# Pairing the spilled U-block outputs of a PEER feed-forward: one tile, one DRAM place and one transfer for two blocks

## The chip, the cores and the metric

The kernel runs on 1 core of one Trainium2 chip. The metric is the device time of one execution in microseconds (us). The kernel before the change was timed three times; the profile is one further execution, taken by the hardware profiler. TensorE does the matrix products (PE in the profile, its weight loads PEld), VectorE and ScalarE (DVE, ACT) the element-wise work, GpSimd (POOL) issues the gathers and SyncE (SP) issues most transfers. SP executes nothing but its issues, strictly in the order of the program: an issue that waits holds all that stand behind it.

## The reference

The reference is one layer of an encoder on 512 tokens of width 1024: two kinds of attention, a projection, a layer norm, and then a PEER feed-forward, a sigmoid gate and a last layer norm. The change touches the PEER part alone:

```python
q = (xb @ w_q).reshape(PEER_CHUNK, PEER_HEADS, PEER_KEY_DIM)
s1 = jnp.einsum('thd,kd->thk', q[..., :half], sub_keys[0])
s2 = jnp.einsum('thd,kd->thk', q[..., half:], sub_keys[1])
v1, i1 = lax.top_k(s1, PEER_TOPK)
v2, i2 = lax.top_k(s2, PEER_TOPK)
...
idx = (e1 * PEER_N_KEYS + e2).reshape(PEER_CHUNK, PEER_HEADS * PEER_TOPK)
g = jax.nn.softmax(cv.astype(jnp.float32), axis=-1).reshape(PEER_CHUNK, -1).astype(xb.dtype)
u = u_table[idx]
hpre = jnp.einsum('td,ted->te', xb, u)
act = g * jax.nn.gelu(hpre, approximate=False)
return jnp.einsum('te,ted->td', act, v_table[idx])
```

Each token picks 128 of 16384 experts (8 heads, 16 each). Expert e has a row of `u_table` and a row of `v_table`, each of 1024 numbers. The result of a token is the sum, over its picks, of the pick's weight g times gelu(token . u row) times the v row.

## The kernel before, in words

**Dense and gathered tokens.** For the first 128 tokens the picked rows are gathered, one row for each token and pick (lines 1351 and 1366), and VectorE does the products (lines 1357 and 1368). For the other 384 tokens (`N_D`) the kernel multiplies with all experts: it scatters the weights g into a dense table (128 blocks of 128 experts, `g_dram`, line 1024), and multiplies that table, times the gelu of the U products, with all of V. Of those 384, the U products of 128 (`N_S`) are gathered earlier as well (`own_rows`), so that the U blocks are made for 256 tokens (`N_U`).

**The lead stage** (415 to 900 us of the profile). For U blocks 0 to 99 (`LEAD`) `lead_block` multiplies one block of U rows with the 256 tokens (line 1150), beside the routing and the building of the dense table; `leave_u` takes the gelu on ScalarE (line 1132) into a tile of 128 experts x 256 tokens, 128 KB. Blocks 0 to 87 (`SPILL`) are then stored in DRAM by ScalarE's own queue (line 1134, `ge_dram`). Blocks 88 to 95 (`KEPT`) stay in tiles of another pool, and blocks 96 to 99 stay in tiles named `ge`. In this stage the order of the work is written out by hand on all engines: a planner (`run_pe`) interleaves matrix products with VectorE's steps by their costs.

**The output stage** (900 to 1518 us). The main loop takes the 128 blocks in the order 88 to 127, then 0 to 87; n is the place in that order. In this loop VectorE's and SP's orders are those of the program; ScalarE's and TensorE's are set by the scheduler that builds the kernel. For place n:

- SP issues, in this order, quarters of the next group's dense table (`load_g`, line 1321; 384 KB each, four for 8 blocks, from place 40 on at n % 8 = 6, 6, 7 and 7), V's block n (`load_v`, line 1336; 512 KB), and the gelu tile `GE_AHEAD` = 3 places on (line 1427; 128 KB; from place 37 to place 124).
- VectorE multiplies the table's block with the gelu tile (line 1432); ScalarE and VectorE split V's block and the product into two parts of fewer bits (lines 99 and 100: `v_hi`, `v_lo` or `whi`, `wlo`, and `a_hi`, `a_lo`).
- TensorE adds 18 products of 128x128 with 128x512 into six accumulators (line 1383).
- At places 8 to 35, `expert_in` makes U block n + 92 (100 to 127), whose gelu tile (line 805) is used four places later.
- VectorE and GpSimd do some of the gathered tokens' rows.

**Buffers.** The name `ge` has `GES` = 9 tiles of 128 x 256 numbers, used in turn by the lead stage, by `expert_in` and by the loads of line 1427. V's blocks have three tiles of `v_raw` and, at odd places from 37 to 123, three of `raw`, so that from place 37 on a load of V waits for the split six places before. The halves `v_hi`, `v_lo`, `a_hi`, `a_lo` have two tiles each.

Of the kernel before, what the change touches and what calls it, by code (L numbers as in the profile page):

```python
# [9 lines left out]
F32 = mybir.dt.float32  # L10
# [4 lines left out]
AF = mybir.ActivationFunctionType  # L15
# [17 lines left out]
N_U = N_D - N_S  # L33
# [3 lines left out]
SPILL = 88  # L37
# [19 lines left out]
NA_FROM = (0, 64, 192, 256)  # L57
GATS = 8
NO_GATHER = 1
GE_AHEAD = 3  # L60
GES = 9
RAWS = 4
LOW = -3.0e38
FEED_NA = 3.1
# [8 lines left out]
def tile_encoder_layer(ctx: ExitStack, tc: tile.TileContext, A: dict, out: bass.AP):  # L73
    nc = tc.nc
# [6 lines left out]
    dram = ctx.enter_context(tc.tile_pool(name="dram", bufs=1, space=bass.MemoryType.DRAM))  # L81
# [14 lines left out]
    def split(hi, lo, src, scale=None):  # L96

        if scale is None:
            nc.scalar.copy(hi, src)  # L99
            nc.vector.tensor_tensor(lo, src, r32(hi), op=OP.subtract)  # L100
        else:
            nc.scalar.mul(hi, src, scale)
            nc.vector.scalar_tensor_tensor(lo, src, scale, r32(hi), op0=OP.mult, op1=OP.subtract)

    def stream(src, shape, scale=None):
        raw = wst.tile([128] + shape, F32, name="raw", bufs=3)
        nc.sync.dma_start(raw, src)
        hi = wst.tile([128] + shape, F32R, name="whi")
        lo = wst.tile([128] + shape, F32R, name="wlo")
        split(hi, lo, raw, scale)  # L110
        return hi, lo

    def mm3(ps, a, b, start, stop):
        nc.tensor.matmul(ps, a[0], b[0], start=start, stop=False)  # L114
        nc.tensor.matmul(ps, a[0], b[1], start=False, stop=False)  # L115
        nc.tensor.matmul(ps, a[1], b[0], start=False, stop=stop)  # L116
# [55 lines left out]
    def ps_tile(name, bufs=2):  # L172
        return ps6.tile([128, 512], F32, name=name, bufs=bufs)
# [102 lines left out]
    with tc.tile_pool(name="ln0", bufs=1, reuse_waits="tile") as ln0, \  # L276
# [16 lines left out]
        for kk in range(4):  # L293
            raw = wst.tile([128, 2, 512], F32, name="raw", bufs=3) if kk < 3 else ln0.tile([128, 2, 512], F32,
                                                                                         name="vraw3")
# [465 lines left out]
    for c in range(4):  # L761
        cs = slice(c * 128, (c + 1) * 128)
        ps = ps_tile("pj")
# [8 lines left out]
    for c in range(4):  # L772
        cs = slice(c * 128, (c + 1) * 128)
        ps = ps_tile("mm")
# [10 lines left out]
    NTG = N_D // GT  # L785
    ts = slice(T - N_U, T)
    u_rows, v_rows = A["u_rows"], A["v_rows"]
    ge_dram = dram.tile([SPILL, 128, N_U], F32, name="ge_dram")
    g_dram = dram.tile([NTG, 128, 128 * GT], F32, name="g_dram")

    pB = ctx.enter_context(tc.tile_pool(name="pB", bufs=1, reuse_waits="tile"))
# [3 lines left out]
    hdot = pB.tile([128, NGC, 128], F32, name="hdot")  # L795
    ge_t = {}

    def expert_in(i):

        ps = psH.tile([128, 512], F32, name="hp")  # L800
        u = stream(A["uT"][i], [8, 128])
        for k in range(8):
            mm3(ps[:, :N_U], (u[0][:, k], u[1][:, k]), (hTh[:, k, ts], hTl[:, k, ts]), k == 0, k == 7)
        ge = pB.tile([128, N_U], F32, name="ge", bufs=GES)
        nc.scalar.activation(ge, ps[:, :N_U], AF.Gelu)
        if i < SPILL:
            nc.sync.dma_start(ge_dram[i], ge)
        else:
            ge_t[i] = ge


    pX = ctx.enter_context(tc.tile_pool(name="pX", bufs=1, reuse_waits="tile"))
# [52 lines left out]
    for g in range(16):  # L865
# [5 lines left out]
        ps = ps_tile("mm", 4)  # L871
# [251 lines left out]
    def leave_u(i, ps):  # L1123
        k = i - SPILL
        if 0 <= k < KEPT:
            if k % 2 == 0:
                name = ("g_raw", "g_raw", "g_hi", "g_lo")[k // 2]
                kept.append(pK.tile([128, 2, N_U], F32, name=name, bufs=2 if k < 4 else 1))
            ge = kept[k // 2][:, k % 2]
        else:  # L1130
            ge = pB.tile([128, N_U], F32, name="ge", bufs=GES)
        nc.scalar.activation(ge, ps[:, :N_U], AF.Gelu)  # L1132
        if i < SPILL:
            nc.scalar.dma_start(ge_dram[i], ge)
        else:
            ge_t[i] = ge

# [71 lines left out]
    def gate_and_leads():  # L1209
# [37 lines left out]
        if last:  # L1247
            leave_u(*last.pop())
# [60 lines left out]
    order = list(range(SPILL, 128)) + list(range(SPILL))  # L1309
    pV = ctx.enter_context(tc.tile_pool(name="pV", bufs=1, side="right", reuse_waits="tile"))  # L1310

    def load_g(n, q, t):

        i = order[n]
        if q == 0:
            if n // GB % 2 == 0:
                t = pX.tile([128, NTG, GB, GT], F32, name="gt1")
            else:
                t = pV.tile([128, NTG, GB, GT], F32, name="gt0")
        g = slice(q * NTG // 4, (q + 1) * NTG // 4)  # L1320
        nc.sync.dma_start(t[:, g].rearrange("p g i t -> p g (i t)"),
                          g_dram[g, :, i * GT:(i + GB) * GT].rearrange("g p x -> p g x"))
        return t

    def block_of_u(n):

        i = n - KEPT + LEAD
        return i if LEAD <= i < 128 else None

    def in_wst(n):  # L1330

        return n % 2 and KEPT + 128 - LEAD < n < 124

    def load_v(n):
        raw = wst.tile([128, D], F32, name="raw", bufs=3) if in_wst(n) else pV.tile([128, D], F32, name="v_raw", bufs=3)
        nc.sync.dma_start(raw, v_rows[order[n] * 128:(order[n] + 1) * 128, :])
        return raw
# [40 lines left out]
    def expert_out(x, c, halves=(0, 1)):  # L1378
        n, ah, al, vh, vl = x
        cs = slice(c * 128, (c + 1) * 128)  # L1380
        for i, (a, b) in enumerate(((ah, vh), (ah, vl), (al, vh))):
            for hf in halves:
                nc.tensor.matmul(acc[c][hf], a[:, cs], b[:, hf * 512:(hf + 1) * 512],  # L1383
                                 start=(n == 0 and i == 0), stop=(n == 127 and i == 2))
# [12 lines left out]
    with tc.manual_schedule(engines={nc.vector.engine, nc.sync.engine}):  # L1397
        for n, i in enumerate(order):
            if n % GB == 0:
                gt = gt_next  # L1400
            if n < 128 - GB:
                for q in range(4):
                    if n % GB == (GB // 2 - 1 + q if n < KEPT + 128 - LEAD + 4 else GB - 2 + q // 2):
                        gt_next = load_g(n // GB * GB + GB, q, gt_next)
            if n not in v_cut:
                raw = v_next.pop(n, None) or load_v(n)
            if n in v_cut:
                vh, vl = v_cut[n]
                ah = pO.tile([128, N_D], F32R, name="a_hi")
                al = pO.tile([128, N_D], F32R, name="a_lo")  # L1410
            elif n in (124, 125):
                vh = wst.tile([128, D], F32R, name="whi")
                vl = wst.tile([128, D], F32R, name="wlo")
                a2 = wst.tile([128, 2, N_D], F32R, name="raw", bufs=3)
                ah, al = a2[:, 0], a2[:, 1]
            else:
                if in_wst(n):
                    vh = wst.tile([128, D], F32R, name="whi")
                    vl = wst.tile([128, D], F32R, name="wlo")
                else:  # L1420
                    vh = pP.tile([128, D], F32R, name="v_hi")
                    vl = pP.tile([128, D], F32R, name="v_lo")
                ah = pO.tile([128, N_D], F32R, name="a_hi")
                al = pO.tile([128, N_D], F32R, name="a_lo")
            if 0 <= n + GE_AHEAD - (128 - SPILL) < SPILL:
                ge = pB.tile([128, N_U], F32, name="ge", bufs=GES)
                nc.sync.dma_start(ge, ge_dram[order[n + GE_AHEAD]])
                ge_t[order[n + GE_AHEAD]] = ge
            ge = ge_t.pop(i)
            a = gt[:, :, n % GB, :]  # L1430
            dn = gt[:, N_S // GT:, n % GB, :]
            nc.vector.tensor_tensor(dn, dn, ge.rearrange("p (g t) -> p g t", t=GT), op=OP.mult)  # L1432
            if n not in v_cut:
                split(vh, vl, raw)
            split(ah.rearrange("p (g t) -> p g t", t=GT), al.rearrange("p (g t) -> p g t", t=GT), a)
            late.append((n, ah, al, vh, vl))
            if n < 124:
                for c in range(NDC):
                    expert_out(late[0], c)
                late = []  # L1440
            u = block_of_u(n)
            if u:
                expert_in(u)
            if n >= NO_GATHER:
                spent += 1 if u else LATE
            upto = min(len(steps), PRE + math.ceil((len(steps) - PRE) * spent / (128 - (1 - LATE) * LEAD - 3 - NO_GATHER)))
            for f in steps[done:upto]:
                f()
            done = upto
        for c in range(NDC):  # L1450
            for hf in range(2):
                for x in late:
                    expert_out(x, c, (hf,))
# [101 lines left out]
```

## Time and profile before

| | |
|---|---|
| median of 3 runs | 1543.56 us (1542.36 to 1547.03) |
| the profiled execution's own time | 1539.35 us |
| its span | 1537.3 us |
| mean granted clock | 0.994 |
| PE busy | 1497.5 us, 97% |
| DVE busy | 1304.3 us, 85% |
| ACT busy | 658.9 us, 43% |
| POOL busy | 559.5 us, 36% |
| moved by the DMA queues | 459.38 MB |

How to read the views. The page gives, for each engine, busy time and share of the span, then the span in 40 slices as tenths. The chain of work that ended last is followed back from the last instruction, at each step to what released it; a DMA on it counts from its issue to its landing. In the chain in order of time a row is start, length, what. In the windows a row gives, for each engine, busy time and number of instructions, then the granted clock of TensorE (1.00 is full), the mean busy share of the 16 DMA engines, and GB/s. In the timeline a row is start, length, engine and line, operation, output<-inputs, shapes, and in brackets the idle time before it and what ended that. A tile's view gives the shortest, the median and the longest duration in ns and the first and the last start. In the DMA view a queue's row gives its packets, its MB and the time that its packets took as a share of 16 engines; q1 is SP's queue, q10 ScalarE's and q0 GpSimd's gathers.

### The profile page before, as it was taken

The numbers are of one execution on the slowest core, as the hardware profiler recorded it, in microseconds if no ns is written. First come the engines' busy times: TensorE is split into PE (matmuls) and PEld (weight loads), VectorE is DVE, ScalarE is ACT, GpSimd is POOL, SyncE is SP. The second block draws the span as 40 slices with busy tenths as digits, with TensorE's granted clock in tenths as the row PEclk, the third lists the DMA queues.
The fourth block names the chain that finished last, engine by engine and source line by source line (L and its number), as shares of the span: only waits on it lengthen the run. The fifth ranks groups of instructions, "written<-read, shape, count | busy, mean of one in ns | idle before, by whom it ended". The sixth has DMA issues, their size and how long they took to land.

```text
span 1537.3 us, 23029 instructions
## 1 busy us (share of the span) xinstructions
PE 1497.5 (97%) x7747; PEld 1255.2 (82%) x7747; DVE 1304.3 (85%) x3022; ACT 658.9 (43%) x1226; POOL 559.5 (36%) x520
## 2 busy tenths in 40 slices
PE   9999899999999999999999999999999999999997
PEld 5788777788888889899889887988987888877885
DVE  6376685679989998898989968989998999889996
ACT  3355685333222665157516533434433333333342
POOL 1013110010015434353314344655555666656620
PEclk9999999999999999999999999999999999999999
DMA  6333340143379999999999999999999999999982
GB/s 228 101 110 96 83 124 29 45 138 89 110 230 339 341 406 384 411 410 413 413 351 383 416 376 373 406 400 393 406 399 394 396 395 395 395 397 388 396 317 77
DMA packets 194218, 459.38 MB, mean 299 GB/s; under 512 B 18226, under 2 KB 97970, under 8 KB 192564
## 3 DMA queue, kind: packets, MB, share of 16 engines
q1 hardware_dynamic: 121712, 214.08, 38.6%
q0 software_dynamic: 57984, 207.12, 35.1%
q10 hardware_dynamic: 14404, 36.71, 6.1%
q8 instruction: 61, 1.00, 0.3%
q14 instruction: 57, 0.47, 0.1%
HBM read 414.07 MB, written 40.89 MB: 296 GB/s over the span
## 4 chain that ended last, share of the span: by engine, by line
PE 66%; DVE 13%; DMA 13%; issue 4%; ACT 2%; POOL 1%; SPq 0%; DVEq 0%; ACTq 0%; POOLq 0%
PE acc L1383 27%; PE hp L1150 5%; PE mm L1150 4%; PE mm L114 3%; PE pj L114 3%; PE mm L116 3%; PE mm L115 3%; DMA raw<-in_v_rows_dram 3%; PE pj L115 3%; PE pj L116 3%; PE tr L1008 3%; DMA row<-in_u_rows_dram,s_ix 3%; DMA whi<-in_u_rows_dram,s_ix 2%; DMA ge<-ge_dram 2%; DVE oh_j L1046 2%
## 5 line engine op out<-in xcount | busy, mean ns | idle before, releaser
L1366 POOL DMA_INDIRECT gat<-in_v_rows_dram,i_sel x128 | 216.7, 1693 | 130.6 <-DVE base L1368 109.2
L1150 PE MATMUL mm<-whole,raw 128*128 128x256 f32 x832 | 187.1, 379 | 1.0 <-DMA raw<-in_uT_dram 1.0
L99 ACT CAST whi<-raw 128x1024 fp32r<-128x1024 f32 (+4 forms) x117 | 117.3, 1003 | 164.4 <-DMA raw<-in_v_rows_dram 51.4
L1351 POOL DMA_INDIRECT gat<-in_u_rows_dram,i_sel x102 | 130.7, 1281 | 119.5 <-DVE hdot L1357 79.4
L1150 PEld LDWEIGHTS mm<-whole,raw 128*128 128x128 f32 x832 | 155.9, 190 | 21.4 <-ACT ge L1132 1.4
L1368 DVE SCALAR_TENSOR_TENSOR base<-gat,hdot,base 128x1024 f32<-128x1024 f32 x128 | 164.1, 1282 | 1.6
L100 DVE TENSOR_TENSOR wlo<-raw,whi 128x1024 fp32r<-128x1024 f32 (+4 forms) x117 | 135.7, 1161 | 33.2 <-ACT whi L99 32.9
L1383 PE MATMUL acc<-v_hi,a_hi 128*128 128x512 f32 x480 | 151.3, 396 | 7.4 <-ACT a_hi L99 6.6
L1383 PE MATMUL acc<-v_lo,a_hi 128*128 128x512 f32 x480 | 150.0, 393 | 0.2
L1383 PE MATMUL acc<-v_hi,a_lo 128*128 128x512 f32 x480 | 149.4, 392 | 0.0
L99 ACT CAST v_hi<-v_raw 128x1024 fp32r<-128x1024 f32 x80 | 83.9, 1050 | 124.5 <-DMA v_raw<-in_v_rows_dram 43.9
L99 ACT CAST a_hi<-gt 128x384 fp32r<-128x384 f32 x126 | 64.5, 512 | 167.3 <-DVE gt L1432 81.3
L1357 DVE CUSTOM_DVE_ANT_0 scr<-gat,h 128x1024 f32<-128x1024 f32 x102 | 124.8, 1224 | 5.5 <-DMA gat<-in_u_rows_dram,i_sel 3.2
L1063 POOL DMA_INDIRECT whi<-in_u_rows_dram,s_ix x51 | 53.7, 1054 | 202.8 <-DVE cand L911 132.3
L1046 DVE TENSOR_SCALAR oh_j<-iota,eT 128x128 f32<-128x128 f32 x384 | 114.8, 374 | 0.0
L1383 PEld LDWEIGHTS acc<-v_hi,a_hi 128*128 128x128 f32 x480 | 88.4, 190 | 26.9 <-ACT a_hi L99 8.7
L1383 PEld LDWEIGHTS acc<-v_lo,a_hi 128*128 128x128 f32 x480 | 90.5, 189 | 21.4 <-DVE v_lo L100 1.8
L1383 PEld LDWEIGHTS acc<-v_hi,a_lo 128*128 128x128 f32 x480 | 90.2, 189 | 20.0 <-DVE a_lo L100 0.5
L100 DVE TENSOR_TENSOR v_lo<-v_raw,v_hi 128x1024 fp32r<-128x1024 f32 x80 | 97.6, 1220 | 8.2 <-ACT v_hi L99 8.2
L100 DVE TENSOR_TENSOR a_lo<-gt,a_hi 128x384 fp32r<-128x384 f32 x126 | 69.9, 555 | 40.2 <-ACT a_hi L99 38.4
L1008 PEld LDWEIGHTS tr<-oh_i,oh_j 128*128 128x128 f32 x768 | 94.1, 191 | 8.6 <-ACT g_st L1020 2.4
L1008 PE MATMUL tr<-oh_i,oh_j 128*128 128x128 f32 x768 | 96.4, 277 | 3.6 <-DVE oh_j L1046 2.6
(394 smaller groups left out, 3510.7 us busy)
## 6 DMA issues: line engine op xcount, KB each, us to landing
raw<-in_uT_dram SPq DMA_DIRECT2D x104, 512.0 KB
v_raw<-in_v_rows_dram SPq DMA_DIRECT2D x82, 512.0 KB
g_dram<-g_st ACTq DMA_DIRECT2D x12, 2048.0 KB
gt<-g_dram SPq DMA_DIRECT2D x60, 384.0 KB
raw<-in_v_rows_dram SPq DMA_DIRECT2D x44, 512.0 KB
raw_u<-in_uT_dram SPq DMA_DIRECT2D x24, 512.0 KB
ge_dram<-ge ACTq DMA_DIRECT2D x88, 128.0 KB
ge<-ge_dram SPq DMA_DIRECT2D x88, 128.0 KB
```

Source lines behind the costliest of these rows:

```text
L99: nc.scalar.copy(hi, src)
L100: nc.vector.tensor_tensor(lo, src, r32(hi), op=OP.subtract)
L114: nc.tensor.matmul(ps, a[0], b[0], start=start, stop=False)
L115: nc.tensor.matmul(ps, a[0], b[1], start=False, stop=False)
L1008: nc.tensor.matmul(ps[:, i * 128:(i + 1) * 128], oj[:, 4 * r + i, :], oi[:, 4 * r + i, :], start=True, stop=True)
L1046: nc.vector.tensor_scalar(oj[:, i], iota, eT[:, 1, t0 + i:t0 + i + 1], eT[:, 2, t0 + i:t0 + i + 1], op0=OP.is_equal, op1=OP.mult)
L1150: nc.tensor.matmul(ps[:, :N_U], raw[:, k], whole[:, k, :], start=(k == 0), stop=(k == 7))
L1351: nc.gpsimd.indirect_dma_start(out=u[:], out_offset=None, in_=u_rows, in_offset=bass.IndirectOffsetOnAxis(ap=i_sel[:, c, k:k + 1], axis=0))
L1357: nc.vector.tensor_tensor_reduce(scr, u, h[c], op0=OP.mult, op1=OP.add, accum_out=hdot[:, c, k:k + 1], scale=1.0, scalar=0.0)
L1366: nc.gpsimd.indirect_dma_start(out=u[:], out_offset=None, in_=v_rows, in_offset=bass.IndirectOffsetOnAxis(ap=i_sel[:, c, k:k + 1], axis=0))
L1368: nc.vector.scalar_tensor_tensor(base[c], u, hdot[:, c, k:k + 1], base[c], op0=OP.mult, op1=OP.add)
L1383: nc.tensor.matmul(acc[c][hf], a[:, cs], b[:, hf * 512:(hf + 1) * 512], start=(n == 0 and i == 0), stop=(n == 127 and i == 2))
```

## The change

The name `ge` now stands for pairs: `GES` = 4 tiles of 128 x 2 x 256 numbers, each with the outputs of two neighbouring blocks. A new helper, `ge_half`, hands out the halves: it takes a new tile for an even block and gives the second half of the same tile for the odd one. `ge_dram` has half as many places of twice the size, so that a partition's two halves stand next to each other (2048 B where there were 1024 B).

In the lead stage each block's gelu goes to its half, and the store is issued once, after the odd block. In `expert_in` the pairs are used in the same way, without a store (that branch, for blocks under 88, never ran there and is gone). In the output stage the load is issued at even places only, for the blocks four and five places on: one load of 256 KB into a new pair. With four pairs in turn, the pair that is taken at place n held the blocks of places n - 4 and n - 3, and so the load waits for the product of line 1432 at place n - 3; with nine single tiles it was that of place n - 6. The first load is issued at place 36 (37 before), the last at place 122 (124 before).

```diff
-GE_AHEAD = 3
-GES = 9
+GE_AHEAD = 4
+GES = 4
...
-    ge_dram = dram.tile([SPILL, 128, N_U], F32, name="ge_dram")
+    ge_dram = dram.tile([SPILL // 2, 128, 2 * N_U], F32, name="ge_dram")
...
+    pair = None
+
+    def ge_half(i):
+
+        nonlocal pair
+        if i % 2 == 0:
+            pair = pB.tile([128, 2, N_U], F32, name="ge", bufs=GES)
+        return pair[:, i % 2]
+
...
-        ge = pB.tile([128, N_U], F32, name="ge", bufs=GES)
-        nc.scalar.activation(ge, ps[:, :N_U], AF.Gelu)
-        if i < SPILL:
-            nc.sync.dma_start(ge_dram[i], ge)
-        else:
-            ge_t[i] = ge
+        ge_t[i] = ge_half(i)
+        nc.scalar.activation(ge_t[i], ps[:, :N_U], AF.Gelu)
...
-            ge = pB.tile([128, N_U], F32, name="ge", bufs=GES)
+            ge = ge_half(i)
         nc.scalar.activation(ge, ps[:, :N_U], AF.Gelu)
         if i < SPILL:
-            nc.scalar.dma_start(ge_dram[i], ge)
+            if i % 2:
+                nc.scalar.dma_start(ge_dram[i // 2], pair.rearrange("p a t -> p (a t)"))
...
-            if 0 <= n + GE_AHEAD - (128 - SPILL) < SPILL:
-                ge = pB.tile([128, N_U], F32, name="ge", bufs=GES)
-                nc.sync.dma_start(ge, ge_dram[order[n + GE_AHEAD]])
-                ge_t[order[n + GE_AHEAD]] = ge
+            m = n + GE_AHEAD - (128 - SPILL)
+            if 0 <= m < SPILL and m % 2 == 0:
+                ge_t[m], ge_t[m + 1] = ge_half(m), ge_half(m + 1)
+                nc.sync.dma_start(pair.rearrange("p a t -> p (a t)"), ge_dram[m // 2])
```

## The prediction, as it went on record

> **What bounds the kernel now.** I read the page first, then the chain of work in order of time, the windows of the output stage, the tile view of `ge`, SP's timeline and SP's waits.
>
> ```profile
> PE 1497.5 (97%) x7747; PEld 1255.2 (82%) x7747; DVE 1304.3 (85%) x3022; ACT 658.9 (43%) x1226; POOL 559.5 (36%) x520
> PE 66%; DVE 13%; DMA 13%; issue 4%; ACT 2%; POOL 1%; SPq 0%; DVEq 0%; ACTq 0%; POOLq 0%
> ```
> ```profile
> 1132.03 16.76 DMA ge<-ge_dram
> 1148.81 9.63 DMA ge<-ge_dram
> 1158.45 1.73 SPq L1321
> 1160.30 14.61 DMA raw<-in_v_rows_dram
> 1176.49 189.84 PE acc L1383 x817
> 1366.33 16.46 DMA raw<-in_v_rows_dram
> 1384.38 133.80 PE acc L1383 x571
> ```
> ```profile
> 1140.00:1160.00 20.00, 18.61 (x81) 14.79 (x80) 16.87 (x23) 9.72 (x13) 10.95 (x7) 1.00 1.04 398
> 1160.00:1180.00 20.00, 17.41 (x70) 13.87 (x69) 15.34 (x19) 5.90 (x8) 10.70 (x7) 0.91 1.04 394
> 1380.00:1400.00 20.00, 17.16 (x68) 13.55 (x67) 15.54 (x19) 6.98 (x10) 10.78 (x7) 0.91 1.02 379
> 400.00:900.00 500.00, 494.14 (x2637) 437.52 (x2637) 443.79 (x1280) 233.69 (x540) 170.95 (x159) 1.00 0.95 363
> 1176.00:1480.00 304.00, 300.67 (x1290) 243.68 (x1291) 281.07 (x331) 106.99 (x145) 189.24 (x110) 0.99 1.04 394
> ```
>
> TensorE bounds the program, and in the last part of the output stage nearly nothing is free: from 1176 to 1480 TensorE is busy 300.67 of 304 us, VectorE 281.07, and the DMA engines show a share of 1.04 throughout. Whatever is lost there ends the program later. The chain has four long DMA pieces between 1132 and 1384, two of them the very loads that the change merges, and TensorE's gaps lie beside them: 20 - 18.61 = 1.39, 20 - 17.41 = 2.59 and 20 - 17.16 = 2.84 us. The last two windows also show a clock of 0.91, as if 9% of 20 us, 1.8 us each, were lost besides. So 6.82 + 3.6 = 10.4 us is all that freer loads could give back there.
>
> A DMA piece of the chain goes from issue to landing, and one row ends where the next issue begins: the `ge` load of 1132.03 lands at 1148.79 and the next piece's issue is at 1148.81. In SP's timeline that is the eighth issue after it:
>
> ```profile
> 1132.03 0.32 SPq L1427 DMA_DIRECT2D ge<-ge_dram  x1
> 1133.75 0.33 SPq L1336 DMA_DIRECT2D raw<-in_v_rows_dram  x1
> 1136.57 0.32 SPq L1427 DMA_DIRECT2D ge<-ge_dram  x1
> ...
> 1147.21 0.33 SPq L1336 DMA_DIRECT2D v_raw<-in_v_rows_dram  x1
> 1148.81 0.32 SPq L1427 DMA_DIRECT2D ge<-ge_dram  x1
> ```
> ```profile
> SPq L1336 <- DMA raw<-in_v_rows_dram: 34.1, 21, 2.9
> SPq L1427 <- DMA ge<-ge_dram: 23.2, 26, 1.3
> SPq L1336 <- DVE v_lo L100: 12.2, 6, 2.8
> ```
>
> I read this as a limit of eight transfers under way: an issue waits until the eighth before it has landed. The waits from 1176 to 1480 say the same: SP mostly waits for landed DMAs, which guard no buffer of the waiting issue, and seldom for a buffer (`v_lo`, 12.2 us).
>
> **The change part by part.**
>
> ```profile
> L1432 DVE TENSOR_TENSOR gt<-gt,ge x120: 416/420/428, 932.4 to 1515.4; 128x256 f32<-128x256 f32 x120
> L1134 ACTq DMA_DIRECT2D ge_dram<-ge x88: 325/326/362, 416.3 to 836.2; - x88
> L1427 SPq DMA_DIRECT2D ge<-ge_dram x88: 319/424/3153, 1115.2 to 1485.2; - x88
>   DMA ge_dram<-ge: 6.1, 2
> ```
>
> *Stores.* 88 issues on ScalarE become 44: 44 x 0.326 = 14.3 us less of ScalarE's time. In 400 to 900 it is busy 233.69 of 500 us, while TensorE is busy 494.14, so the cover is TensorE's work; all that is not covered is 5.9 us of TensorE gaps, whatever causes them. I count 0, bounds -1 and 0. The store of a pair leaves one block later and its tile is wanted again seven blocks on, not nine. A block takes (836.2 - 416.3) / 87 = 4.8 us, so 34 us are left; ScalarE waited for a store twice, 6.1 us in all, off the path. 0 again.
>
> *Bytes and packets.* The bytes stay; the pieces double from 1 to 2 KB. Three rows give the prices (the stretch 620 to 660 for 1 KB on q10 and 4 KB on q0, the stretch 15 to 20 for 2 KB on q1):
>
> ```profile
> q0 software_dynamic: 2262, 8.23, 50.8%
> q10 hardware_dynamic: 1955, 1.77, 12.8%
> ```
> ```profile
> q1 hardware_dynamic: 572, 1.07, 60.6%
> ```
>
> q10: 0.128 x 16 x 40 us for 1.77 MB is 46 ns per KB. q0: 0.508 x 640 / 8.23 is 40 ns per KB. The 2 KB row gives 0.606 x 80 / 1.07 = 45, from one load and one store of 256 KB. I take 42, nearer to the 4 KB row, which ran under the same load. A pair is 262 KB: 262 x 4 ns / 16 engines = 0.066 us saved, plus its second transfer's 16 small completion packets; 0.07 in all, so 44 x 0.07 = 3.1 us for the loads and as much for the stores. It counts only where the DMA engines are on the path. In the output stage that is 16.76 + 9.63 + 14.61 + 16.46 = 57.5 of the 388 us from 1130 to the chain's last matrix product at 1518 (1384.38 + 133.80), 15%: **-0.5 us** (bounds -3.1 and 0). For the stores I take 0 (bounds -3.1 and 0).
>
> *Slots.* Two places issued two V loads, two `ge` loads and one quarter of the table: five issues. Now they are four, so eight slots reach four places instead of 3.2. What that can give is bounded by the 10.4 us; I take 0, since with the engines at 1.04 a transfer issued sooner stands longer in the queue.
>
> *Order in the queue.* The pair stands ahead of V blocks that formerly had one or two `ge` loads fewer before them: 131 to 262 KB, once. The rate of q1 in 1180 to 1360 is 36.32 MB / 180 us = 202 GB/s:
>
> ```profile
> q1 hardware_dynamic: 20554, 36.32, 54.5%
> ```
>
> So V comes 0.65 to 1.3 us later, in the stretch from 1115 where the chain runs through DMAs: **+0.7 us** (bounds 0 and 1.3).
>
> *The new wait.* At every even place n the `ge` issue waits for VectorE's product at n - 3, not n - 6. Behind it on SP stand V's block n + 1, at every fourth such place two quarters of the table, and V's block n + 2; TensorE waits for those in the end. Count line 1432's rows from block 8: its 50th, 52nd and 54th are blocks 57, 59 and 61, its 102nd is block 109. SP's rows are those of blocks 60 and 61, then one quarter pair, block 63 and block 109.
>
> ```profile
> 1211.97 0.33 SPq L1336 DMA_DIRECT2D v_raw<-in_v_rows_dram  x1
> 1212.35 0.43 SPq L1427 DMA_DIRECT2D ge<-ge_dram  x1
> 1215.11 0.33 SPq L1336 DMA_DIRECT2D raw<-in_v_rows_dram  x1
> ...
> 1225.06 3.48 SPq L1321 DMA_DIRECT2D gt<-g_dram  x2
> 1228.65 1.67 SPq L1336 DMA_DIRECT2D raw<-in_v_rows_dram  x1
> ...
> 1419.34 0.33 SPq L1336 DMA_DIRECT2D raw<-in_v_rows_dram  x1
> ```
> ```profile
> 1223.11 0.42 DVE L1432 TENSOR_TENSOR gt<-gt,ge 128x256 f32<-128x256 f32 x1
> 1231.07 0.42 DVE L1432 TENSOR_TENSOR gt<-gt,ge 128x256 f32<-128x256 f32 x1
> 1239.37 0.42 DVE L1432 TENSOR_TENSOR gt<-gt,ge 128x256 f32<-128x256 f32 x1
> ...
> 1443.28 0.42 DVE L1432 TENSOR_TENSOR gt<-gt,ge 128x256 f32<-128x256 f32 x1
> ```
>
> V's block 61 was issued at 1215.11, 24.3 us before its product at 1239.37. Under the change the issue ahead of it waits until 1223.53, so it goes out at about 1224.0: 8.9 us later, 15.4 us ahead of use. V's block 60, issued at 1211.97, had landed by the eighth issue after it, 1225.06 (the first of that row's two), so the queue is nearly empty when SP is let go: here the delay costs transfer time. From 1224.0 to V's block 63 the queue then has two pairs (524 KB), three V blocks (1573 KB) and four quarters (1573 KB): 3.67 MB / 202 GB/s = 18.2 us, so 1242.2, and 2 to 3 us to land (estimated from the chain's 9.63 us for a load with about 7 us of work ahead of it): 1244 to 1245. Before, block 63 (1228.65) was down 14.6 to 16.8 us later by the chain's rows, 1243.3 to 1245.4. So -1 to +2 us, about +1. Where the queue still holds work while SP waits, the delay costs nothing. That is the common case: a load takes 14.6 to 16.8 us to land, the hold is mostly under 9. The quarters come in bursts, begun right after V's block with n % 8 = 5, in ten groups from block 45 to 117. In two of the ten SP was as far ahead as here: at block 61, and at block 109, issued 23.9 us before its product (1443.28 - 1419.34). 2 x 1 = **+2 us**. Lower bound 0; upper bound ten bursts at 2 us, 20.
>
> *Sum.* -0.5 + 0.7 + 2 = +2.2 us on the profiled execution's 1539.35 (span 1537.3 and 2.05 around it): 1541.55. The median of the runs is 4.21 above that execution: **1545.8 us**, +0.14%, inside the 0.3% (4.6 us) that a measurement of this kernel can tell from no change.
>
> **The rivals.**
>
> *Faster: the loads stop binding.* With a fifth fewer issues the slots no longer hold SP from 1132 to 1175 and at 1366. For it: two `ge` loads make 26.4 us of the chain, and the chain passes from one to the next by a slot. Against it: the DMA share of 1.04. It gives back most of 10.4 us and 0.5 of packets: about -10, 1534. The Trainium skill speaks for it (Perfetto Trace Analysis, DMA Optimizations): transfers in pieces under 2 KB carry much overhead, and merging is the first remedy when DMA binds. Its page DMA: Bandwidth & Descriptors (Bandwidth) has the same in a fit, about 2 us fixed per DMA plus the bytes, by which 44 loads fewer would save an estimated 88 us if they ran one by one. The rows do not bear that out: the issues of 1132 to 1149 overlap eight deep.
>
> *Slower: SP's hold decides.* Each table burst, entered with V 15.4 us ahead instead of 20 or more, has V's last block of the group (n % 8 = 7) late by 1 to 2 us, and VectorE, busy 281 of 304 us, cannot win it back. It decides as soon as a load takes more than about 13 us after its now later issue, and the chain's rows are 14.6 and more. Ten bursts at 1.2 us: +12, 1555. The skill supports the mechanism (DMA: Bandwidth & Descriptors, Anatomy of one DMA): a wait is served on the issuing sequencer before dispatch, so what stands behind it is not even queued. Against it: with fewer issues the queue is shorter and a load lands sooner.
>
> *It does not do what it says:* ScalarE's order in the output stage is the scheduler's, and may come out otherwise with other transfers; either sign, inside the range.
>
> **How the numbers follow.** Forecast 0.42, faster rival 0.27, slower rival 0.31; the third is spread over these. The range takes in most of both rivals, from 1534.5 to 1557: the sum's upper bound of 20 us is left out beyond the slower rival's 12, as it needs every burst late. Chances: faster 0.27, same 0.42, slower 0.31.
>
> **What would show it.** Right: 44 issues of line 1134 and about 44 of the load, 256 KB each; SP waiting for line 1432's product at the pair's load; odd V blocks issued about 15.5 us before their product; TensorE's gaps after 1130 summing to some 5 to 10 us as before. The faster rival: no gaps after 1130, no `ge` on the chain. The slower: gaps, or late `a_hi`, at n % 8 = 6 and 7 in most groups. Wrong altogether: a shift in the lead stage, where I count nothing.

## The result, and the profile after

The changed kernel takes 1565.75 us (median of 6 runs, 1559.17 to 1570.24), against 1542.64 (1539.88 to 1547.03) for six runs of the kernel before beside it: 1.0146 times as long, 95% interval 1.012 to 1.0172. Forecast was 1545.8, no change, with a range up to 1557. The profiled execution of after took 1559.17 us (span 1557.1, mean clock 0.989). It is the fastest of the six, so the account below is of the 19.8 us between the two profiled executions, not of the 23.1 between the medians. In after the code lies some lines lower: the table's load is line 1327, V's load 1342, the pair's load 1434, the product 1438, the matrix products 1389.

The page of after, busy times and the chain by engine:

```profile
PE 1503.1 (97%) x7747; PEld 1256.5 (81%) x7747; DVE 1302.1 (84%) x3022; ACT 657.4 (42%) x1226; POOL 558.4 (36%) x520
PE 50%; DVE 20%; DMA 18%; issue 9%; ACT 3%; POOL 1%; SPq 0%; DVEq 0%; ACTq 0%; POOLq 0%
```

The work is the same, but DMA's share of the chain has grown from 13% to 18% and TensorE's has fallen from 66% to 50%. The windows of after, of 20 us each, that lose anything between 1120 and 1480, and the two long ones that the prediction read:

```profile
1140.00:1160.00 20.00, 14.44 (x55) 11.28 (x54) 13.14 (x19) 6.69 (x9) 8.73 (x5) 0.83 0.90 341
1240.00:1260.00 20.00, 17.18 (x75) 13.48 (x74) 13.61 (x17) 5.45 (x7) 9.66 (x6) 1.00 0.90 336
1280.00:1300.00 20.00, 16.47 (x61) 12.87 (x61) 14.52 (x19) 6.99 (x9) 10.04 (x6) 0.83 0.96 360
1360.00:1380.00 20.00, 18.17 (x79) 14.48 (x78) 17.28 (x21) 8.48 (x11) 10.76 (x7) 1.00 0.95 353
1380.00:1400.00 20.00, 16.36 (x70) 12.68 (x68) 13.12 (x16) 4.79 (x7) 9.93 (x6) 0.99 1.03 393
1400.00:1420.00 20.00, 19.74 (x74) 15.84 (x74) 19.63 (x23) 7.47 (x12) 12.82 (x8) 0.84 0.87 322
400.00:900.00 500.00, 492.08 (x2626) 435.83 (x2625) 441.07 (x1278) 232.25 (x539) 168.91 (x159) 1.00 0.94 362
1176.00:1480.00 304.00, 291.93 (x1237) 234.17 (x1236) 263.10 (x310) 101.84 (x136) 182.21 (x107) 0.98 0.99 375
```

These rows account for the loss. The product of place 36 starts at 1134.09 us in after and 1133.17 in before: the lead stage has cost 0.9 us. That of place 127 starts at 1535.17 against 1515.4: the output stage has cost 18.8 more. TensorE's idle time in the six short windows is 5.56 + 2.82 + 3.53 + 1.83 + 3.64 + 0.26 = 17.64 us, and two windows after 1480 add 1.19; before had 6.82. That is 12.0 us more. Three windows ran at a clock of 0.83 to 0.84 and one at 0.99, 20 x (0.17 + 0.17 + 0.16 + 0.01) = 10.2 us, where before lost 3.6: 6.6 more. Together 18.6 of 18.8. The DMA share says what kind of loss it is: before held 1.02 to 1.05 throughout, and here it drops to 0.87 to 0.96 in five of the six. By the packets of the trace, SP's queue had none under way for 18.9 of the 304 us from 1176 to 1480, against 0.7 us in before: it has run dry, a us or two at a time.

The chain in order of time, from 1160 us:

```profile
1169.67 12.30 DMA raw<-in_v_rows_dram
...
1237.47 15.24 DMA raw<-in_v_rows_dram
1274.35 15.65 DMA raw<-in_v_rows_dram
...
1311.87 13.25 DMA raw<-in_v_rows_dram
1346.77 14.27 DMA raw<-in_v_rows_dram
1382.69 15.99 DMA raw<-in_v_rows_dram
...
1455.48 12.65 DMA raw<-in_v_rows_dram
...
1490.89 12.18 DMA raw<-in_v_rows_dram
```

The `ge` pieces are gone from it, but for one of 3.97 us at 1506.76. Instead V's last block of a group of eight places (n % 8 = 7) stands there, in eight of the ten groups from block 47 to 119. In the nine groups from block 47 to 111 this block always landed after the product of the place before its own, by 1.2 to 6.1 us; in before that was so in six of the nine, by 0.6 to 4.5. SP's waits of after from 1176 to 1480 (us in total, times, longest) say why:

```profile
SPq L1434 <- DVE gt L1438: 216.7, 34, 12.3
SPq L1342 <- ACT a_hi L99: 11.5, 24, 2.4
SPq L1434 <- DMA ge<-ge_dram: 2.6, 3, 1.3
```

SP waits for a slot hardly at all any more; over two thirds of its time it stands at the pair's load, for the product that frees the pair. One group of after: SP's timeline, with V's blocks 67 to 72 (from 1258.13 on, one row each of `raw` or `v_raw`), then VectorE's products of blocks 63, 65 and 67, then ScalarE and TensorE.

```profile
1244.52 0.38 SPq L1342 DMA_DIRECT2D v_raw<-in_v_rows_dram  x1
1257.72 0.33 SPq L1434 DMA_DIRECT2D ge<-ge_dram  x1
1258.13 0.39 SPq L1342 DMA_DIRECT2D raw<-in_v_rows_dram  x1
1258.61 0.38 SPq L1342 DMA_DIRECT2D v_raw<-in_v_rows_dram  x1
1265.31 0.33 SPq L1434 DMA_DIRECT2D ge<-ge_dram  x1
1265.73 0.38 SPq L1342 DMA_DIRECT2D raw<-in_v_rows_dram  x1
1266.21 0.92 SPq L1327 DMA_DIRECT2D gt<-g_dram  x2
1267.17 0.70 SPq L1342 DMA_DIRECT2D v_raw<-in_v_rows_dram  x1
1272.91 0.33 SPq L1434 DMA_DIRECT2D ge<-ge_dram  x1
1273.28 0.97 SPq L1327 DMA_DIRECT2D gt<-g_dram  x2
1274.35 1.19 SPq L1342 DMA_DIRECT2D raw<-in_v_rows_dram  x1
1275.63 3.00 SPq L1342 DMA_DIRECT2D v_raw<-in_v_rows_dram  x1
```
```profile
1257.27 0.42 DVE L1438 TENSOR_TENSOR gt<-gt,ge 128x256 f32<-128x256 f32 x1
...
1264.86 0.42 DVE L1438 TENSOR_TENSOR gt<-gt,ge 128x256 f32<-128x256 f32 x1
...
1272.46 0.42 DVE L1438 TENSOR_TENSOR gt<-gt,ge 128x256 f32<-128x256 f32 x1
```
```profile
1290.07 1.04 ACT L99 CAST whi<-raw 128x1024 fp32r<-128x1024 f32 x1 [6.73 <-DMA raw<-in_v_rows_dram]
1291.03 0.51 ACT L99 CAST a_hi<-gt 128x384 fp32r<-128x384 f32 x1
```
```profile
1291.58 1.22 PE L1389 MATMUL acc<-v_hi,a_hi 128*128 128x512 f32 x2 [3.53 <-ACT a_hi L99]
```

Each pair's load goes out within 0.5 us of a product: SP now goes at VectorE's pace. Between 1244.9 and 1257.72 it issues nothing. By 1257.72 the queue has nearly run out, as block 67's landing shows: issued at 1258.13, down 5.3 us later, where V's loads take 11 to 15 us in before, by the mean of each n % 8. Then most of a group's work comes in 18 us: three pairs, six V blocks and four quarters of the table. So block 71 is issued at 1274.35 and lands 15.65 us later, at 1290.00. ScalarE takes things in its own order, and there the split of block 71 stands ahead of `a_hi` of block 70. Block 70's product was ready at 1286.4 + 0.4, its `a_hi` starts at 1291.03, and TensorE, idle for 3.53 us, then runs its next products at half speed (1.22 us for a pair that takes 0.63 otherwise).

The stores and loads themselves are as forecast, 44 each, and the packets' time barely moves: q1's share is 38.6% of 1537.3 us before and 38.2% of 1557.1 after, 593 and 595 us.

### The profile page after: what moved, and what is told of

Read it like the earlier page. It is cut to its first block, busy times and chain, and to the rows that moved or that the text cites. A ratio compares the mean times of both kernels' runs of the same rounds, so it can differ in the third digit from the quotient of the medians.

```text
span 1557.1 us, 22931 instructions
## 1 busy us (share of the span) xinstructions
PE 1503.1 (97%) x7747; PEld 1256.5 (81%) x7747; DVE 1302.1 (84%) x3022; ACT 657.4 (42%) x1226; POOL 558.4 (36%) x520
## 3 DMA queue, kind: packets, MB, share of 16 engines
q1 hardware_dynamic: 115376, 214.07, 38.2%
## 4 chain that ended last, share of the span: by engine, by line
PE 50%; DVE 20%; DMA 18%; issue 9%; ACT 3%; POOL 1%; SPq 0%; DVEq 0%; ACTq 0%; POOLq 0%
PE acc L1389 12%; DMA raw<-in_v_rows_dram 7%; PE hp L1156 4%; DMA row<-in_u_rows_dram,s_ix 4%; PE mm L114 3%; PE mm L1156 3%; PE pj L114 3%; PE mm L116 3%; PE mm L115 3%; DVE base L1374 3%; PE pj L115 3%; PE pj L116 3%; PE tr L1013 3%; DMA wlo<-in_u_rows_dram,s_ix 2%; DMA raw<-in_uT_dram 2%
## 5 line engine op out<-in xcount | busy, mean ns | idle before, releaser
L1389 PE MATMUL acc<-v_hi,a_hi 128*128 128x512 f32 x480 | 155.1, 404 | 21.7 <-ACT a_hi L99 21.5
L1156 PEld LDWEIGHTS mm<-whole,raw 128*128 128x128 f32 x832 | 155.9, 190 | 20.8 <-issue 0.8
```

The lines of the kernel that those rows point to most:

```text
L1156: nc.tensor.matmul(ps[:, :N_U], raw[:, k], whole[:, k, :], start=(k == 0), stop=(k == 7))
```

## The experiments

Theory 1: SP's hold costs. The wait for the product of n - 3 lets the queue run empty in every group, and V comes late. Theory 2: pairing itself costs (larger transfers ahead of V, or another order on ScalarE). Each ratio is to runs of the kernel before on the same chip.

**Undoing the wait in three ways, and making it without pairs.** e1 takes a pair two places ahead instead of four; its load then waits for the product of n - 5, not n - 3. e2 is three places ahead (n - 4).

```diff
-GE_AHEAD = 4
+GE_AHEAD = 2
```

> Everything as after the change, but the pair is loaded two and three places ahead instead of four and five. With the same four pairs, the pair taken at place n then held places n - 6 and n - 5, so SP waits for the product at n - 5, which is where V's own buffers hold it anyway. Theory 1 (SP's wait for the product at n - 3 holds V's block and the table's quarters behind it, about 2 us lost in each of ten groups of eight blocks): the loss goes, 1538 to 1546 us, V's odd blocks issued 20 us or more before their product instead of 14 to 16. Theory 2 (the pair itself: one transfer of 256 KB in front of V instead of two of 128 KB apart, or ScalarE's order that the scheduler set anew): still 1558 to 1570.

> Everything as after the change, but three and four places ahead: the load is issued at odd places and waits for the product at n - 4. One place less of hold. Theory 1: between the two kernels and near the one before, 1541 to 1553 us, odd leads of about 19 to 20 us for the block behind the wait. Theory 2: still 1558 to 1570.

e3 keeps four places and the wait for n - 3, but ScalarE issues the load, so that nothing of SP's stands behind it.

```diff
-                nc.sync.dma_start(pair.rearrange("p a t -> p (a t)"), ge_dram[m // 2])
+                nc.scalar.dma_start(pair.rearrange("p a t -> p (a t)"), ge_dram[m // 2])
```

> Everything as after the change, same pairs, same wait for the product at n - 3, but the pair's load of the output stage is issued by ScalarE and not by SP. The wait stays, and what is queued behind it is no longer V's blocks. Theory 1: the loss goes, 1537 to 1547 us, unless ScalarE itself is held up by the wait (then late casts, and slower). Theory 2: still 1558 to 1570, since transfers and sizes are the same.

e4 is the kernel before, without pairs, with six single tiles: each load waits for n - 3.

```diff
-GES = 9
+GES = 6
```

> The kernel before, unpaired, three places ahead, with 6 single tiles instead of 9: each load of a gelu tile waits for the product at n - 3. No pairing, only the wait, now at every place. Theory 1: V's blocks issued about 16 us ahead at every place, as slow as after the change or slower, 1560 to 1585 us. Theory 2: as before, 1540 to 1546.

Measured: e1 1544.24 us, 1.002 (1.0001 to 1.004); e2 1544.94, 1.0032 (1.0011 to 1.0053); e3 1544.39, 1.0017 (0.999 to 1.0043); e4 1581.22, 1.0263 (1.0226 to 1.0299). SP's waits and the window from 1176 to 1480 of e1, then the same of e4:

```profile
SPq L1434 <- DVE gt L1438: 72.9, 28, 5.0
SPq L1342 <- DVE v_lo L100: 66.2, 24, 4.8
```
```profile
1176.00:1480.00 304.00, 304.00 (x1320) 246.97 (x1320) 283.77 (x334) 109.09 (x147) 188.27 (x113) 1.00 1.04 399
```
```profile
SPq L1427 <- DVE gt L1432: 169.2, 53, 9.8
```
```profile
1176.00:1480.00 304.00, 279.23 (x1161) 222.77 (x1160) 252.25 (x298) 95.85 (x129) 171.36 (x102) 0.96 0.97 357
```

With pairs and no long hold TensorE has no gap at all in this window and the DMA share is 1.04 (e1's one gap, 4.53 us, ends at 1144.78); with the hold and no pairs the loss is larger than after's. Theory 2 falls. e3 shows where the wait has to stand to hurt: the same wait, on a queue with no V behind it, costs nothing that can be told from the error.

**More of the wait.** e10 is after with `GE_AHEAD = 5`: the same ring, the pair's load a place earlier, waiting for n - 2.

```diff
-GE_AHEAD = 4
+GE_AHEAD = 5
```

> The kernel after with GE_AHEAD = 5: the same ring of four pairs, the pair's load one place earlier still, at odd places, so that it waits for the product of n - 2. Theory 1 (each pair's wait holds SP, the queue runs empty, and what stands behind comes later by a block, 3.9 us): the V block behind the wait is issued 11 to 12 us before its product instead of 15, and the loss of about 2 us in a group of eight blocks becomes about 6: 1600 to 1620 us. Rival (the loss of after is the price of the bursts alone and does not grow with the wait): 1563 to 1575 us.

1598.41 us, 1.0362 (1.0337 to 1.0388): just below the theory's range, far outside the rival's. Its waits and its window:

```profile
SPq L1434 <- DVE gt L1438: 215.9, 31, 13.6
```
```profile
1176.00:1480.00 304.00, 278.40 (x1133) 220.20 (x1132) 244.49 (x288) 94.36 (x127) 166.34 (x98) 0.95 0.94 345
```

The total of SP's waiting is that of after (215.9 and 216.7 us), and the loss is two and a half times as large. In these six kernels the loss goes with how far ahead of its product a V block is still issued. The table has, for places 44 to 115, this lead from the issue of V's block to the product of line 1432 or 1438; then the time in which SP's queue had no packet under way from 1176 to 1480; and the time that the profiled execution took from place 36 to 127 beyond before's:

| kernel | shortest lead, us | blocks under 16 us, of 72 | queue without a packet, us | places 36 to 127, us more |
|---|---|---|---|---|
| before | 18.1 | 0 | 0.7 | 0 |
| e1 (n - 5) | 20.2 | 0 | 0.4 | -3.6 |
| e2 (n - 4) | 16.5 | 0 | 1.6 | -2.8 |
| after (n - 3) | 14.3 | 19 | 18.9 | +18.8 |
| e4 (n - 3, every place) | 13.3 | 34 | 12.3 | +30.0 |
| e10 (n - 2) | 9.9 | 46 | 50.4 | +48.1 |

Between 16.5 and 14.3 us the loss sets in here; from 1160 to 1500 us, a V load on after's chain takes 12 to 16 us, and it must be down before `a_hi` of the place ahead of its own.

**Is it the burst of the table's quarters behind the hold?** e5 is after with one quarter at each of n % 8 = 3, 4, 5, 6. e7 and e8 do the same to before and to e1, where it might save the remaining gaps.

```diff
-                    if n % GB == (GB // 2 - 1 + q if n < KEPT + 128 - LEAD + 4 else GB - 2 + q // 2):
+                    if n % GB == GB // 2 - 1 + q:
```

> The kernel after with the table's four quarters at one place each (n % 8 = 3, 4, 5, 6) in the whole output stage, instead of two and two at n % 8 = 6 and 7. Theory 1a (the hold costs at every even place, because q1 runs empty while SP waits for the product of n - 3): the time stays where it is, 1560 to 1570 us, and odd V blocks are still issued 15 to 17 us before their product. Theory 1b (the slower rival as the prediction put it: the hold costs only because a burst of quarters stands right behind it): a group's blocks 6 and 7 land in time, and the time falls to 1543 to 1550 us.

> The kernel before (single loads of ge, three places ahead) with the table's quarters at one place each. Theory A (in before the table's bursts cost nothing that matters: the queue is full and the engines are the limit): 1539 to 1546 us. Theory B (the gaps of 1.4 to 2.8 us after 1130 us and the half clock behind them come from bursts that hold V back): up to 10 us faster, 1532 to 1538 us.

> The kernel of e1_ahead2 with the table's quarters at one place each: pairs without the long hold and without bursts, the version that should be the best of the pairs. Theory A: as e1_ahead2, 1540 to 1547 us. Theory B: up to 10 us faster, 1532 to 1538 us.

e5: 1555.35 us, 1.0084 (1.0054 to 1.0114), between the two expectations. e7: 1549.63, 1.0053 (1.0032 to 1.0073), and e8: 1557.72, 1.0097 (1.0071 to 1.0123), both slower where the same or faster was expected. SP's first wait of e7 and its timeline show what I had overlooked:

```profile
SPq L1321 <- DVE a_lo L100: 64.9, 9, 10.3
```
```profile
1278.63 0.43 SPq L1427 DMA_DIRECT2D ge<-ge_dram  x1
1288.28 0.37 SPq L1321 DMA_DIRECT2D gt<-g_dram  x1
1288.70 0.49 SPq L1336 DMA_DIRECT2D raw<-in_v_rows_dram  x1
```

The quarter, issued three places earlier, waits for the table's buffer, still read by `a_lo` of the group before: nine holds of 7.2 us in the mean, with V behind them. So e7 has no pairs and no wait for n - 3, and it loses time by a hold on another buffer; its shortest lead is 12.7 or 14.0 us, once in a group. It cannot say what the bursts are worth alone. Why e8 with its pairs is the slower of the two stays open. But e5 against after says that part of after's loss, about 0.6 of the 1.5%, goes when the burst no longer stands behind the third hold, although e5 has gained a hold of its own.

**What is the merge worth by itself?** e6 is e1 with two loads of half a pair, one behind the other.

```diff
-                nc.sync.dma_start(pair.rearrange("p a t -> p (a t)"), ge_dram[m // 2])
+                for j in range(2):
+                    nc.sync.dma_start(ge_t[m + j], ge_dram[m // 2][:, j * N_U:j * N_U + N_U])
```

> The kernel of e1_ahead2 (no long hold), but each pair is loaded by two transfers of half a tile in 1 KB pieces, issued one behind the other: 88 loads again, everything else as in e1. It measures what merging the loads is worth by itself. Theory 1 (the merge is worth nothing here, since the DMA engines are full and the slots only decide who waits): within 4 us of e1_ahead2, 1541 to 1548 us. Rival (the 44 loads fewer and 2 KB pieces gave something that e1 shows no gain from because its holds ate it): 5 to 12 us slower than e1_ahead2, 1549 to 1556 us.

1546.78 us, 1.0028 (1.0011 to 1.0046), where e1 had 1.002 (1.0001 to 1.004): about 1 us for 44 loads fewer, with both intervals at most some 5. From place 36 to 127 the two profiles show no gain at all (-3.9 us for e6, -3.6 for e1).

**The stores.** e9 is e1 with each half stored by itself, e11 is e3 with the same.

```diff
-            if i % 2:
-                nc.scalar.dma_start(ge_dram[i // 2], pair.rearrange("p a t -> p (a t)"))
+            j = i % 2 * N_U
+            nc.scalar.dma_start(ge_dram[i // 2][:, j:j + N_U], ge)
```

> The kernel of e1_ahead2 (pairs loaded together, no long hold), but each half of a pair is stored by itself as soon as it is made: 88 stores in 1 KB pieces again. In the profiles of the kernels that store pairs, block 36 of the output stage comes 0.9 to 10.4 us later than in before (median 6.5 of seven), and from block 36 to the end those without the long hold take 3 to 4 us less than before. Theory S (storing pairs costs in the lead stage what loading pairs gives in the output stage): block 36 within 2 us of before, and the time 2 to 5 us under before: 1537 to 1540 us. Theory 1 (stores cost nothing either way, and the lead stage differs from run to run): as e1_ahead2, 1542 to 1546 us.

> The kernel of e3_actq (pairs loaded from ScalarE's queue, the wait for the product of n - 3 kept there), with single stores as in e9_ahead2_1store. Theory S: 1537 to 1540 us, the best of all versions. Theory 1: as e3_actq, 1541 to 1546 us.

e9: 1538.08 us, 0.9976 (0.9962 to 0.999). e11: 1541.13, 0.9984 (0.9969 to 0.9999). By their ratios both are under before and under their twins with stored pairs, as theory S has it. But e11's time lies in theory 1's range, and the profiles have block 36 4.2 us late in e9 and 11.1 in e11, which theory S does not allow. So four kernels were set side by side: e13 is e1 again, e14 is e9 again, e15 stores two halves but both after the second, and e16 is after with single stores.

```diff
+            for j in range(2 if i % 2 else 0):
+                nc.scalar.dma_start(ge_dram[i // 2][:, j * N_U:j * N_U + N_U], pair[:, j])
```

> The kernel of e1_ahead2 once more, beside the three others on one chip, since e1_ahead2 and e9_ahead2_1store were timed against before in two different jobs. Theory S (a stored pair costs): 1.001 to 1.004 of before, as e1. Theory N (the two differ by what differs between jobs): 0.997 to 1.000.

> The kernel of e9_ahead2_1store once more on the same chip: single stores, loaded pairs, no long hold. Theory S: 0.996 to 0.999 of before and 4 to 8 us under e13_ahead2_again. Theory N: within 3 us of e13_ahead2_again.

> The kernel of e1_ahead2 with the pair stored as two halves in 1 KB pieces, but both issued together after the second half is made. It tells the size of the pieces from the time of the store. If the merged transfer with its 2 KB pieces costs: as e14_ahead2_1store_again. If it costs that the first half waits a block and 262 KB then enter the queues at once: as e13_ahead2_again. Theory N: all three within 3 us of each other.

> The kernel after with single stores, its loads and its wait for the product of n - 3 unchanged. Theory S: of the loss of 1.5%, 0.35 to 0.45 is the stores', so 1.010 to 1.012 of before; the rest, about 17 us, stays with the hold. Theory N: as after, 1.013 to 1.017.

e13: 1543.01 us, 1.0003 (0.9986 to 1.002). e14: 1539.06, 0.9983 (0.9968 to 0.9998). e15: 1539.56, 0.9991 (0.9977 to 1.0005). e16: 1572.22, 1.0178 (1.0152 to 1.0203). e13 and e14 are 4 us apart, as theory S has it, though e13 is no slower than before, which is nearer theory N; e15 lies with e14, which would put it on the merged transfer; and e16 contradicts theory S outright: single stores do not make after faster, its ratio is above after's. So a stored pair is worth between 0 and some 7 us to the worse without the hold (the two pairs of ratios differ by 0.0044 and 0.002), and no price of it holds in all kernels. That stays open. e9, measured twice, is the fastest version found, by 0.2%: less than the 0.3% that I named as the bound for one measurement, though 1 lies outside both intervals.

**Singles from ScalarE's queue.** e12 is before with line 1427 issued by ScalarE.

```diff
-                nc.sync.dma_start(ge, ge_dram[order[n + GE_AHEAD]])
+                nc.scalar.dma_start(ge, ge_dram[order[n + GE_AHEAD]])
```

> The kernel before (single tiles, ring of nine, three places ahead) with the loads of ge issued by ScalarE instead of SP. If what e1 and e3 gain after block 36 comes from SP having fewer issues and slots to pass and not from merged transfers, this kernel gains it too: 3 to 4 us under before, 1537 to 1540 us. If it comes from the merge: as before, 1540 to 1544 us. ScalarE then carries 88 issues of 0.33 us more, 29 us, which may cost a few us: up to 1548 us.

1550.07 us, 1.0048 (1.0031 to 1.0065): slower, beyond every expectation, with V's shortest lead at 18.7 us and a mean of 23.6, where before has 20.8. So a longer lead of V alone brings nothing. The trace offers a cause, in the slowest of its six runs only: ScalarE is held at its own `ge` loads (from 1270.3 to 1275.5 and from 1277.4 to 1282.9 us, until transfers had landed), an `a_hi` stands behind each, and TensorE is then idle for 3.09 us, to 1283.96. No run tests it.

**What the lead does not give.** It does not order all kernels. e5, with a shortest lead of 12.7 us and 20 blocks under 16, took 12.5 us more from place 36 to 127, less than after; e7 and e8 (12.7; 13 and 10 blocks) 6.9 and 10.9; e12, with none under 16, 7.6. e16, whose output stage is after's, took 26.6 where after took 18.8. So the lead tells that a kernel loses, and only roughly how much.

## Why the prediction was wrong, point by point

**The new wait is the step that failed**, in its size: +2 us in the sum. The prediction saw the wait for n - 3, and V and the table behind it on SP. It worked the case of blocks 61 to 63 out to +1 us, with a lead of 15.4 us for block 61 (after: 14.3). But block 63, which came down 1.0 us after the product of block 62 in before, came down 6.1 us after it in after: 5 us, not 1. Then it said: "Where the queue still holds work while SP waits, the delay costs nothing. That is the common case", and counted two bursts of ten. This was read from before's trace, where a load takes 14.6 to 16.8 us to land because SP issues early. The wait takes away just that: SP's queue stood without a packet for 18.9 us from 1176 to 1480, and V's last block was late in every group from 47 to 111. The measured size is +15.8 us from place 48 to 127, the other 3.0 of the 18.8 being there by place 48. e1, e3 and e4 show that the wait alone makes it, e10 that it grows with the wait.

The prediction's upper bound, ten bursts at 2 us, 20, comes near, but partly by luck. Every burst was late, and yet TensorE stood still only where the late block used up all the work that TensorE had left: behind the products of places 62, 70, 86 and 94 (2.81, 3.53, 1.83 and 0.95 + 2.95 us, with half speed behind the second and the last) and by 1.19 us behind 117 and 118. At places 46, 54, 78, 102 and 110 it lost nothing.

**The slower rival had the mechanism and two thirds of its size**: a late V block in each group and late `a_hi` at n % 8 = 6 in most, at 1.2 us for each of ten. The gaps came in half of the groups only, and cost more each. The sentence behind it from the Trainium skill (DMA: Bandwidth & Descriptors, Anatomy of one DMA), that a wait is served on the issuing sequencer before dispatch, agrees with SP's timeline: nothing was issued behind the pair's load for up to 12.3 us, and block 67 then landed in 5.3 us.

**Of the size**, two parts were not in the working at all. V's block is wanted a place earlier than its own product, since ScalarE splits it ahead of the previous block's `a_hi`; the comparison with before's landing hid that. And the clock: 6.6 of the 18.6 us are products at half speed behind the gaps, though the prediction had counted the same loss in before (3.6 us) when it bounded the gain.

**Packets, -0.5**: q1's packet time did not fall (593 to 595 us); e6 puts the merge of the loads at about 1 us, within its error. **Slots, 0**: the slots did stop binding (SP waited 4.1 us for landed transfers in after from 1176 to 1480, 121 in before), and alone they gave nothing: e6 has 88 loads again and is within the error of e1. They are a wait of this program, and the traces show no limit of the queue: nearly each of SP's issues in the output stage (192 of 216 in after) waits for the semaphore that its own transfer will raise, and SP uses eight of them in turn. **The faster rival** got no gain from the merge: 1.002 (1.0001 to 1.004) in e1, where pieces of 1 KB, in loads of 128 KB, became pieces of 2 KB. The Trainium skill (Perfetto Trace Analysis, DMA Optimizations), which it named, has small DMAs, under 2 KB, as the ones with much overhead. Of the 88 us by the fit of the Trainium skill (DMA: Bandwidth & Descriptors) nothing appears. That fit stands in the section Anatomy of one DMA and was measured on DMAs that GpSimd issues; the loads here are SP's, and they overlap. **Order in the queue, +0.7**: place 40 of after comes 4.8 us late where place 36 was 0.9 late, behind the gap of 5.56 us that ends at 1149.83. Other kernels with merged loads lose there too (e1 goes from 5.3 to 8.6 us, e3 from 7.2 to 9.5, e16 from 8.3 to 9.5), and e6 with its half loads does not (8.3 to 7.9). So the first pairs ahead of V cost 1 to 4 us, and the term was too small. **Stores, 0**: right for after as profiled (place 36 at +0.9 us); q10's packet time fell from 94 to 90 us, off the path, much as worked out; for the other kernels open, as said.

**The signs named** held: 44 and 44 issues, SP at the product, odd V blocks about 15 us ahead (mean 16.7, shortest 14.3), no shift in the lead stage (0.9 us). TensorE's gaps summing to 5 to 10 us as before did not: 18.8.

## What to carry to other kernels

When a change makes a buffer ring shorter, write down for each load on an in-order queue what it now waits for, and add the delay to everything behind it before asking whether the queue "still holds work": the landing times of the trace of before were made by the early issues that the wait abolishes. Compare the lead that remains with the landing time under load, and with the place at which another engine's order first needs the data; a pattern that repeats every group comes short in every group, even where the engine that counts has work left and shows no gap. Bigger transfers were worth about 1 us here, within the error; the place of the wait was worth 20.

## What the runs showed of the hardware that was not expected

How long a gap it takes to halve TensorE's clock is not fixed: one of 2.81 us in after was not followed by half speed, one of 2.33 in e10 (ending at 1205.05) was. What decides is how much idle time falls into one window of a fixed grid. In the clock records of all 18 traces the clock changes only on a grid of 3.41 us, whose phase differs from execution to execution, and the slow spells last one or two of its windows, 3.41 or 6.83 us (but for the one at the end of each). From 100 us to 40 us before the end, 7339 windows at full speed were counted. All 76 of them in which TensorE's rows leave more than 1.91 us idle were followed by a window at half speed, none of the 7240 with less than 1.68 was, and of the 23 between, 12 were. So about half a window of idle time was enough, and a gap that is cut by the grid counts for each window by itself. The gap of 2.81 us in after had 1.19 us in one window and 1.63 in the next. In e4 a gap of 4.15 us ended at 1267.06, and its products ran at full speed until the next window began, at 1268.0 (the clock is the third value from the right):

```profile
1264.00:1268.00 4.00, 0.94 (x4) 0.82 (x5) 0.96 (x2) 1.48 (x3) 0.00 (x0) 1.00 1.04 402
1268.00:1271.40 3.40, 3.40 (x10) 2.65 (x9) 3.36 (x4) 1.87 (x3) 2.04 (x2) 0.50 0.35 139
```

The Trainium skill (TensorE: Matmul & The Clock Gate, What's actually happening) has a free-running window of about 3.4 us, idle throughout, before the clock drops. That the window is of this length and runs freely, the records agree with; that a whole idle window is needed, they do not. The ends of the products are modelled and a few per cent of them can be missing from a trace, so the idle times are not exact. One window at half speed costs 1.7 us and two cost 3.4, which is of the order of the gap that they follow.

Kernels whose code is the same up to the first load of a pair reach place 36 of the output stage up to 10 us apart (0.9 us later than before in after, 9.4 in e10, 7.2 in e3); e1 and e13, one program, 5.3 and 3.0. With one profile each, a difference of a few us in the total says nothing about the stage that was changed. The time from place 36 on says more, but it too moves: -5.7 us in e9, and -2.3 in e14, the same program.
